# Outputs of narrow experts: from scatter-adds into DRAM to one-hot products added to sums in SBUF

## The chip, the cores and the metric

The kernel runs on one core of one Trainium2 chip. The metric is the time of one execution in device microseconds (us). Three runs of the kernel before took 1312.32 to 1319.89 us, median 1319.34.

## The reference, cut to what matters

One layer (`DEPTH = 1`) of an encoder on 512 tokens of width 1024: a mixer (sparse and differential attention), cross-attention into 256 memory tokens, and a mixture of experts, each followed by a LayerNorm. The change lies in the experts. Each token goes to 8 of 64 SwiGLU experts:

```python
scores = jax.nn.sigmoid(xf @ router_w)
_, top_e = lax.top_k(scores + router_bias, TOP_K)            # 8 of 64
gates = top_s / jnp.sum(top_s) * ROUTED_SCALE
# per block of rows of one expert e, rows = its tokens, g = their gates
yb = (silu(xb @ w_gate[e]) * (xb @ w_up[e])) @ w_down[e] * g   # 1024 -> 256 -> 1024
acc = acc.at[rows].add(yb)
out = acc + shared_expert(x);   h = layer_norm(ALPHA * h + out)
```

All is float32; the weights of one expert are three matrices of 1 MB.

## The kernel before, in words

The kernel is one program of five engines. A small planner (`schedule`) interleaves generator threads; every `yield a, b` gives a time estimate, and a scheduler then sets each engine's own instruction order. The dense stages fill the first 600 us; from then on the thread `experts` runs one block of rows after another.

Experts are ranked by how many tokens chose them, and each rank has a fixed capacity (`CAPS`): 128 rows for the fullest, then 112, 96, 80, 64 and 48. Two ranks have 160 rows and make two blocks, one of 128 and one of 32 rows; `BIG_AT = (30, 50)` says at which steps of the sequence they stand. So there are 64 steps and 66 blocks.

There are two kinds of block. A **wide** one (over 64 rows, or the second part of a 160-row expert) splits its gate and up weights into a high and a low part (ScalarE, VectorE; `split_w`) and multiplies in three products (`mm3`, lines 101 to 103, `expert_mm`). A **narrow** one (64 or 48 rows; `narrow_block`) multiplies plain float32, gate and up side by side in the two halves of a PSUM bank (`narrow_mm`, line 1280). Either way a block goes: gather of its rows from DRAM (`gather`, line 1220, GpSimd queue), transposes (line 1268 for narrow), gate and up products, SiLU on ScalarE (line 1299, tile `sg`), product with up and gate weight on VectorE (line 1304, `hm`), transposes of `hm` (line 1313) and their copy (line 1315, `ht`), the down product (line 1291 for narrow, 1327 for wide). The last three belong to the block before: `narrow_block` finishes block m-1 between its own products. The result is copied to a tile `y` by ScalarE (line 1294) and added to rows of the DRAM tensor `acc` by an indirect DMA that accumulates (`scatter`, line 1332, GpSimd queue). Two scatters must not overlap, so each waits for the one before to land.

Before the experts the shared expert's output and the residual are stored to `acc` (line 1374). After the last scatter, and a loop over experts that overflow their capacity (no turn with these inputs), `acc` is loaded (line 1625, tile `h`) and the last LayerNorm runs on it (lines 171 to 188, 263 to 269, 1639) and stores the output.

Weights are loaded by SyncE's queue (`load_p`, `load_w`, lines 1226 and 1235). `top_up` keeps it `LEAD = 9` loads (three experts) ahead of the block in work. A load's target is one of 20 slots of 8 KB per partition that all large tiles share: raw weights, split weights, `y`.

Of the kernel before, what the change touches and what calls it, by code (L numbers as in the profile page):

```python
# [10 lines left out]
F32 = mybir.dt.float32  # L11
# [8 lines left out]
P = 128  # L20
SEQ = 512
# [18 lines left out]
AHEAD, LEAD = 2, 9  # L40
BIG_AT = (30, 50)
GRP = 4
# [16 lines left out]
def encoder_layer(  # L59
# [16 lines left out]
    def slot(shape, dt=F32, name="s"):  # L76
        return slots.tile(shape, dt, tag="s", name=name)
# [4 lines left out]
    def bank(name="ps"):  # L82
        return psum.tile([P, 512], F32, tag="ps", name=name)
# [1198 lines left out]

    def narrow_out(m, ht, wd, n):

        if m % 2 == 0:
            Y["y"] = slot([P, 2, D], name="y")
        y = Y["y"][:, m % 2, :]
        ps = bank()
        for j in range(2):
            for c in range(2):  # L1290
                nc.tensor.matmul(ps[HALF * c:HALF * c + n, :], lhsT=ht[:, j, 0:n], rhs=wd[:, j, c * 512:(c + 1) * 512],
                                 start=j == 0, stop=j == 1)
        for c in range(2):
            nc.scalar.copy(y[0:n, c * 512:(c + 1) * 512], ps[HALF * c:HALF * c + n, :])
        return y

# [184 lines left out]
    def finish(m, ht, n, wd, si):  # L1481
        if narrow(m):
            y = narrow_out(m, ht, wd, n)
        else:
            for c in range(2):
                y = expert_out(m, ht, wd, c, n)
        scatter(y, si, n)

# [5 lines left out]
    def narrow_block(m, X, xt, gs, si):  # L1494
        r, _, n, _ = blocks[m]
        step = 3 * step_of[r]
        ps = bank()
        w = W[r]
        narrow_mm(xt, w, n, ps, range(KH))
# [3 lines left out]
        yield 0.9, 0.0  # L1503
# [12 lines left out]
    def experts():  # L1516
# [73 lines left out]
    with tc.For_i(0, left, 1) as k:  # L1590
# [83 lines left out]
```

## Time and profile before

| | before |
|---|---|
| runs, median (range) | 1319.34 us (1312.32 to 1319.89) |
| profiled execution, time | 1310.08 us |
| its span, first to last instruction | 1308.3 us |
| busy: PE, PEld, DVE, ACT, POOL | 1155.8, 908.2, 748.5, 562.0, 439.5 us |
| HBM read, written | 288.10 MB, 35.19 MB |

PE is TensorE's matmuls, PEld its weight loads, DVE VectorE, ACT ScalarE, POOL GpSimd, SP SyncE (which only issues DMAs here). A matmul's row lasts from its start to its modelled end, and the next one starts before that end. DMA is the mean busy share of the core's 16 DMA engines. q0 is the queue of the indirect DMAs (gathers and scatters), q1 that of SP.

### The profile page before, as it was taken

How to read it: one execution, taken by the hardware profiler on the slowest of the kernel's cores; microseconds unless marked ns; L12 is line 12 of the kernel's file. 1: busy time of each engine (PE TensorE's matmuls, PEld its weight loads, DVE VectorE, ACT ScalarE, POOL GpSimd, SP SyncE). 2: the span in 40 equal slices, each digit the busy share in tenths (PEclk: the TensorE clock that was granted, in tenths of full speed). 3: DMA queues.
4: the chain of work that ended last, by engine and by line, in shares of the span. 5: the costliest groups of instructions: out<-in, count | busy, mean ns of one | idle time of the engine just before them, and what ended most of it. 6: DMA issues, size and time to landing. Idle time of an engine off the chain costs nothing. (4 is left out here: it accounts for less than half of the span.)

```text
span 1308.3 us, 20859 instructions
## 1 busy us (share of the span) xinstructions
PE 1155.8 (88%) x7768; PEld 908.2 (69%) x7768; DVE 748.5 (57%) x1617; ACT 562.0 (43%) x1006; POOL 439.5 (34%) x288
## 2 busy tenths in 40 slices
PE   3999999999898899889999999999899988897770
PEld 2887778988898898878778777777667544553330
DVE  7168986566865557787767777666465211311114
ACT  3235456644454453335555556555454211321122
POOL 4333444542236343552212323232213222223213
PEclk9999999998999899999999999999999989998995
DMA  7322234463326256688999999999999999999974
GB/s 225 86 74 65 58 103 114 121 202 116 126 67 210 63 185 208 226 332 329 299 289 331 352 347 362 332 359 359 350 367 338 350 347 387 363 363 353 349 279 141
DMA packets 136807, 324.67 MB, mean 248 GB/s; under 512 B 12001, under 2 KB 94945, under 8 KB 111873
## 3 DMA queue, kind: packets, MB, share of 16 engines
q1 hardware_dynamic: 119984, 275.83, 58.2%
q0 software_dynamic: 13632, 46.80, 14.8%
q8 instruction: 62, 1.02, 0.3%
q10 hardware_dynamic: 3088, 0.69, 0.2%
q14 instruction: 41, 0.33, 0.1%
HBM read 288.10 MB, written 35.19 MB: 247 GB/s over the span
## 5 line engine op out<-in xcount | busy, mean ns | idle before, releaser
L95 POOL TENSOR_TENSOR whl<-wraw,whl 128x1024 fp32r<-128x1024 f32 x81 | 195.9, 2419 | 265.4 <-ACT whl L94 239.4
L1244 DVE TENSOR_TENSOR whl<-wraw,whl 128x1024 fp32r<-128x1024 f32 x152 | 182.9, 1231 | 85.7 <-ACT whl L1243 79.6
L1332 POOL DMA_INDIRECT acc<-y,sidx x66 | 104.8, 1587 | 361.5 <-DMA acc<-y,sidx 161.4
L101 PE MATMUL ps<-whl,xt 128*96 128x256 f32 (+4 forms) x640 | 184.3, 288 | 5.6 <-ACT whl L1243 3.9
L103 PE MATMUL ps<-whl,xt 128*96 128x256 f32 (+4 forms) x640 | 179.8, 281 | 1.9 <-DVE xt L95 1.9
L102 PE MATMUL ps<-whl,xt 128*96 128x256 f32 (+4 forms) x640 | 179.6, 281 | 0.6 <-DVE whl L1244 0.6
L1243 ACT CAST whl<-wraw 128x1024 fp32r<-128x1024 f32 x152 | 152.5, 1053 | 27.9 <-DMA wraw<-in_e_w_gate_dram 20.0
L1327 PE MATMUL ps<-wd,ht 128*96 128x512 f32 (+4 forms) x320 | 147.1, 603 | 4.0 <-DVE ht L1315 3.8
L1280 PE MATMUL ps<-wraw,xn 128*64 128x256 f32 (+1 forms) x832 | 116.8, 404 | 27.0 <-DMA wraw<-in_e_w_up_dram 12.2
L1220 POOL DMA_INDIRECT xg<-rows,gidx x66 | 76.5, 1159 | 160.3 <-PE ps L1252 62.5
L1299 ACT ACTIVATE sg<-ps 64x256 f32<-64x256 f32 (+6 forms) x66 | 25.0, 378 | 239.6 <-PE ps L1280 127.1
L94 ACT CAST whl<-wraw 128x1024 fp32r<-128x1024 f32 x91 | 95.4, 1048 | 57.1 <-PE ps L103 46.5
L101 PEld LDWEIGHTS ps<-whl,xt 128*96 128x96 f32 (+4 forms) x640 | 104.3, 163 | 6.8 <-ACT whl L1243 4.1
L103 PEld LDWEIGHTS ps<-whl,xt 128*96 128x96 f32 (+4 forms) x640 | 104.3, 163 | 2.9 <-DVE xt L95 2.6
L1280 PEld LDWEIGHTS ps<-wraw,xn 128*64 128x64 f32 (+1 forms) x832 | 60.6, 140 | 65.0 <-DMA wraw<-in_e_w_up_dram 15.8
L102 PEld LDWEIGHTS ps<-whl,xt 128*96 128x96 f32 (+4 forms) x640 | 104.5, 163 | 1.1 <-DVE whl L1244 0.7
L1327 PEld LDWEIGHTS ps<-wd,ht 128*96 128x96 f32 (+4 forms) x320 | 49.5, 164 | 72.9 <-issue 66.0
L1315 DVE COPY ht<-ps 128x128 f32<-128x128 f32 (+6 forms) x66 | 21.4, 324 | 96.3 <-PE ps L1313 96.3
L1328 ACT COPY y<-ps 96x512 f32<-96x512 f32 (+4 forms) x80 | 46.3, 582 | 68.8 <-PE ps L1327 67.4
L1304 DVE SCALAR_TENSOR_TENSOR hm<-ps,og,sg 64x256 f32<-64x256 f32 (+4 forms) x54 | 36.8, 681 | 58.0 <-ACT sg L1299 48.8
L101 PE MATMUL ps<-xTh,whl 128*128 128x512 f32 (+1 forms) x168 | 65.6, 390 | 0.0
L103 PE MATMUL ps<-xTh,whl 128*128 128x512 f32 (+1 forms) x168 | 63.8, 380 | 0.0
(421 smaller groups left out, 2756.7 us busy)
## 6 DMA issues: line engine op xcount, KB each, us to landing
wraw<-in_e_w_gate_dram SPq DMA_DIRECT2D x64, 1024.0 KB, 18.8
wraw<-in_e_w_up_dram SPq DMA_DIRECT2D x64, 1024.0 KB, 15.7
wd<-in_e_w_down_dram SPq DMA_DIRECT2D x64, 1024.0 KB, 18.0
wraw<-in_w_in_dram SPq DMA_DIRECT2D x21, 512.0 KB, 3.7
wraw<-in_m_wkv_dram SPq DMA_DIRECT2D x16, 512.0 KB, 4.2
wraw<-in_m_wq_dram SPq DMA_DIRECT2D x16, 512.0 KB, 3.9
wraw<-in_m_wo_dram SPq DMA_DIRECT2D x16, 512.0 KB, 3.9
wraw<-in_w_o_dram SPq DMA_DIRECT2D x12, 512.0 KB, 3.5
```

Source lines behind the costliest of these rows:

```text
L94: nc.scalar.copy(hi, src)
L95: eng.tensor_sub(lo, src, hi.bitcast(F32))
L101: nc.tensor.matmul(ps, lhsT=a, rhs=b, start=start, stop=False)
L102: nc.tensor.matmul(ps, lhsT=a, rhs=bl, start=False, stop=False)
L103: nc.tensor.matmul(ps, lhsT=al, rhs=b, start=False, stop=stop)
L1220: nc.gpsimd.indirect_dma_start(out=xg[0:n, :], out_offset=None, in_=rows, in_offset=bass.IndirectOffsetOnAxis(ap=gi[0:n, :], axis=0))
L1243: nc.scalar.copy(hi[v], w[i][v])
L1244: lo_eng.tensor_sub(lo[v], w[i][v], hi[v].bitcast(F32))
L1280: nc.tensor.matmul(ps[HALF * i:HALF * i + n, 0:256], lhsT=xt[:, k, 0:n], rhs=w[i][:, k, :], start=k == 0, stop=k == KD - 1)
L1327: nc.tensor.matmul(ps[0:n, :], lhsT=ht[:, j, 0:n], rhs=wd[:, j, cs], start=j == 0, stop=j == 1)
L1328: nc.scalar.copy(y[0:n, cs], ps[0:n, :])
L1332: nc.gpsimd.indirect_dma_start(out=acc, out_offset=bass.IndirectOffsetOnAxis(ap=si[0:n, :], axis=0), in_=y[0:n, :], in_offset=None, comput ...
```

## The change

Narrow blocks no longer scatter. The sequence is reordered so that all 26 narrow blocks come last (`BIG_AT = (22, 32)`) and are taken in 13 pairs, two blocks of up to 64 rows filling the 128 partitions of one tile `yp`. Each result is written to `yp` as a high part (ScalarE) and a low part (VectorE). From the two blocks' token numbers (`si`, cast to float in `stf`) VectorE makes a one-hot matrix of 128 rows by 512 tokens. `add_sums` multiplies it with `yp`: for 4 tiles of 128 tokens and 2 halves of the width, two products (high, low) into one PSUM bank, which VectorE adds to sums in SBUF (`ACC`). These sums are loaded from `acc` once, by the GpSimd queue, at the third narrow block, and the last LayerNorm reads them in place. The 8 groups of a pair are queued (`READY`, `FL`) and taken by `flush`: two groups at two places in each block, from the block after the pair's end, and what is left at the end. In the narrow stage weights are loaded 12 ahead, not 9.

```diff
-BIG_AT = (30, 50)
+BIG_AT = (22, 32)
...
+    def start_sums():
+        OHS[0] = ohs = slot([P, 4, SEQ], F32R, name="ohs")
+        tk = wk([P, SEQ], name="tk")
+        nc.gpsimd.iota(tk, pattern=[[1, SEQ]], base=0, channel_multiplier=0, allow_small_or_imprecise_dtypes=True)
+        nc.vector.tensor_copy(ohs[:, 0, :], tk)
+
+    def load_sums():
+        for u in range(2):
+            a = slot([P, 2, D], name="sums")
+            for t in range(2):
+                nc.gpsimd.dma_start(a[:, t, :], acc[(2 * u + t) * P:(2 * u + t + 1) * P, :])
+                ACC.append(a[:, t, :])
+
+    def one_hot_rows(oh, stf):
+        nc.vector.tensor_scalar(oh, OHS[0][:, 0, :].bitcast(F32), stf, None, op0=OP.is_equal)
+
+    def add_sums(oh, yp):
+        for t in range(NT):
+            for c in range(2):
+                cs = slice(c * 512, (c + 1) * 512)
+                ps = bank()
+                for l in range(2):
+                    nc.tensor.matmul(ps, lhsT=oh[:, t * P:(t + 1) * P], rhs=yp[:, l, cs], start=l == 0, stop=l == 1)
+                nc.vector.tensor_add(ACC[t][:, cs], ACC[t][:, cs], ps)
+                yield
...
-    def narrow_out(m, ht, wd, n):
-        if m % 2 == 0:
-            Y["y"] = slot([P, 2, D], name="y")
-        y = Y["y"][:, m % 2, :]
+    def narrow_out(m, ht, wd, n, si):
+        i = m - M0
+        p, base = i // 2, HALF * (i % 2)
+        if i % 2 == 0:
+            PAIR[p] = slot([P, 2, D], F32R, name="yp")
+            STF[p] = small.tile([P, 1], F32, name="stf", bufs=3)
+            if min(blocks[m][2], blocks[m + 1][2]) < HALF:
+                nc.vector.memset(STF[p], -1.0)
+        yp, stf = PAIR[p], STF[p]
+        r = slice(base, base + n)
+        if n < HALF:
+            nc.gpsimd.memset(yp[base + 32:base + HALF].bitcast(F32), 0.0)
         ps = bank()
...
+        nc.scalar.copy(stf[r], si[0:n])
         for c in range(2):
-            nc.scalar.copy(y[0:n, c * 512:(c + 1) * 512], ps[HALF * c:HALF * c + n, :])
-        return y
+            cs, v = slice(c * 512, (c + 1) * 512), ps[HALF * c:HALF * c + n, :]
+            nc.scalar.copy(yp[r, 0, cs], v)
+            nc.vector.tensor_sub(yp[r, 1, cs], v, yp[r, 0, cs].bitcast(F32))
+        if i % 2:
+            oh = OHS[0][:, 1 + p % 3, :]
+            one_hot_rows(oh, STF.pop(p))
+            READY.append(add_sums(oh, PAIR.pop(p)))
...
     def top_up(used):
         ahead = 16 + used // 2 if "listed" in done else 0
-        while fetched[0] < min(max(used + LEAD, ahead), 3 * NEXP):
+        lead = LEAD + (3 if used > 3 * step_of[blocks[M0][0]] else 0)
+        while fetched[0] < min(max(used + lead, ahead), 3 * NEXP):
...
         narrow_mm(xt, w, n, ps, range(KH))
         yield 0.45 * KH, 0.0
         ht = expert_h(*BEFORE[0][0:2])
+        flush(2)
         narrow_mm(xt, w, n, ps, range(KH, KD))
...
             X[m + 1] = rows_x(m + 1)
-        yield 0.8, 0.0
+        flush(2)
+        yield 1.6, 0.0
...
         finish(NB - 1, expert_h(*BEFORE[0][0:2]), *BEFORE[0][1:])
+        FL.extend(READY)
+        flush(16)
...
-    h3 = [slot([P, 2, D], name="h") for _ in range(2)]
-    for t in range(NT):
-        nc.sync.dma_start(h3[t // 2][:, t % 2, :], acc[t * P:(t + 1) * P, :])
...
-        h = h3[t // 2][:, t % 2, :]
+        h = ACC[t]
```

The overflow loop's body is changed in the same way (it has no turn here).

How this moves instructions, at three places. First PE, the last narrow blocks and the end: before (line 1268 transposes of gathered rows, 1280 gate and up, 1313 transposes of `hm`, 1291 down product),

```order
L1268 MATMUL ps<-ident,xg 128x48 x8
L1280 MATMUL ps<-wraw,xn 48x256
L1313 MATMUL ps<-ident,hm 128x48 x2
L1291 MATMUL ps<-wd,ht 48x512 x4
L1280 MATMUL ps<-wraw,xn 48x256 x15
L1313 MATMUL ps<-ident,hm 128x48 x2
L1291 MATMUL ps<-wd,ht 48x512 x4
L1589 TENSOR_LOAD rt
```

and with the change (1366 is the old 1313, 1330 the old 1291, 1310 the one-hot products):

```order
L1268 MATMUL ps<-ident,xg 128x48 x8
L1310 MATMUL ps<-yp,ohs 128x512 x4
L1280 MATMUL ps<-wraw,xn 48x256 x12
L1366 MATMUL ps<-ident,hm 128x48 x2
L1310 MATMUL ps<-yp,ohs 128x512 x4
L1280 MATMUL ps<-wraw,xn 48x256 x4
L1330 MATMUL ps<-wd,ht 48x512 x4
L1310 MATMUL ps<-yp,ohs 128x512 x4
L1366 MATMUL ps<-ident,hm 128x48 x2
L1330 MATMUL ps<-wd,ht 48x512 x4
L1310 MATMUL ps<-yp,ohs 128x512 x24
L1655 TENSOR_LOAD rt
```

Each block has gained 8 products of 512 columns, 4 of them between the transposes of its rows and its first product, and 24 stand after the last down product.

Second POOL, the queue of gathers (1220) and scatters (1332). Before, the end of the kernel,

```order
L1220 DMA xg<-rows,gidx 48x1024
L1332 DMA acc<-y,sidx 640x1024
L1220 DMA xg<-rows,gidx 48x1024 x2
L1332 DMA acc<-y,sidx 640x1024 x2
L1220 DMA xg<-rows,gidx 48x1024 x2
L1332 DMA acc<-y,sidx 640x1024
L1220 DMA xg<-rows,gidx 48x1024
L1332 DMA acc<-y,sidx 640x1024 x7
```

and with the change the whole narrow stage (1385 is the last wide scatter, 1297 the load of the sums, 1326 the zeroing of empty rows):

```order
L1385 DMA acc<-y,sidx 640x1024
L1220 DMA xg<-rows,gidx 64x1024 x2
L1297 DMA sums<-acc 128x1024 x4
L1220 DMA xg<-rows,gidx 64x1024 x12
L1220 DMA xg<-rows,gidx 48x1024 x6
L1326 MEMSET yp 32x2048
L1220 DMA xg<-rows,gidx 48x1024
L1326 MEMSET yp 32x2048 x6
```

Scatters no longer stand between the gathers, and four loads and seven fills are new.

Third DVE at the end: before,

```order
L1315 COPY ht<-ps 128x2x48
L1304 SCALAR_TENSOR_TENSOR hm<-ps,og,sg 48x128x2
L1271 COPY xn<-ps 128x4x48
L1315 COPY ht<-ps 128x2x48
L1304 SCALAR_TENSOR_TENSOR hm<-ps,og,sg 48x128x2
L1315 COPY ht<-ps 128x2x48
L1589 TENSOR_LOAD rt
```

and with the change (1368 is the old 1315, 1311 an addition to the sums, 1336 the low part of `yp`):

```order
L1311 TENSOR_TENSOR sums<-sums,ps 128x512
L1368 COPY ht<-ps 128x2x48
L1336 TENSOR_TENSOR yp<-ps,yp 48x512
L1311 TENSOR_TENSOR sums<-sums,ps 128x512
L1336 TENSOR_TENSOR yp<-ps,yp 48x512
L1311 TENSOR_TENSOR sums<-sums,ps 128x512 x2
L1336 TENSOR_TENSOR yp<-ps,yp 48x512
L1311 TENSOR_TENSOR sums<-sums,ps 128x512 x9
L1655 TENSOR_LOAD rt
```

Behind the last `ht` copy VectorE now has 3 low parts and 12 additions to do.

## Rows read from the trace of the kernel before

**Rows 1.** The page: span, and busy share of the DMA engines in 40 slices.
```profile
span 1308.3 us, 20859 instructions
...
DMA  7322234463326256688999999999999999999974
```

**Rows 2.** Stages: us; busy PE, PEld, DVE, ACT, POOL; clock, DMA share, GB/s.
```profile
602.00:1010.00 408.00, 393.91 (x2707) 307.00 (x2706) 274.18 (x509) 219.69 (x330) 111.82 (x74) 0.99 1.00 343
1010.00:1268.00 258.00, 218.16 (x1471) 116.08 (x1469) 50.60 (x148) 56.00 (x117) 60.72 (x51) 0.93 1.01 357
1268.00:1308.30 40.30, 1.92 (x8) 0.43 (x8) 14.67 (x27) 8.61 (x14) 14.03 (x12) 0.59 0.42 124
```

**Rows 3.** DMA queues, 1107 to 1112 us: packets, MB, share of 16 engines.
```profile
q1 hardware_dynamic: 292, 2.13, 100.8%
```

**Rows 4.** DMA queues, 1216.5 to 1219.0 us: one scatter of 64 rows.
```profile
q0 software_dynamic: 70, 0.26, 52.5%
```

**Rows 5.** DMA queues, 1092.3 to 1094.6 us: one gather of 64 rows.
```profile
q0 software_dynamic: 63, 0.25, 35.3%
```

**Rows 6.** Timeline of PE, one narrow block: start, us, what, [idle before <-releaser].
```profile
1044.39 2.81 PE L1280 MATMUL ps<-wraw,xn 128*64 128x256 f32 x24 [0.26 <-ACT xn L1273]
...
1048.31 1.89 PE L1291 MATMUL ps<-wd,ht 128*64 128x512 f32 x8
1050.12 0.71 PE L1268 MATMUL ps<-ident,xg 64*128 64x64 f32 x8
1051.86 2.81 PE L1280 MATMUL ps<-wraw,xn 128*64 128x256 f32 x24 [1.03 <-ACT xn L1273]
```

**Rows 7.** Timeline of PE: products of 512 columns of split operands, back to back.
```profile
100.11 0.40 PE L101 MATMUL ps<-xTh,whl 128*128 128x512 f32 x1
...
100.81 0.40 PE L101 MATMUL ps<-xTh,whl 128*128 128x512 f32 x1
```

**Rows 8.** Groups by line and shape: VectorE and ScalarE operations; last numbers busy us, mean ns.
```profile
L1294 ACT COPY y<-ps 64x512 f32<-64x512 f32 x38 | 22.0, 579 | 8.6 <-PE ps L1291 8.3
L1304 DVE SCALAR_TENSOR_TENSOR hm<-ps,og,sg 64x256 f32<-64x256 f32 x19 | 12.8, 672 | 24.7 <-ACT sg L1299 24.6
L95 DVE TENSOR_TENSOR x<-ps,x 128x512 fp32r<-128x512 f32 x16 | 10.4, 677 | 0.0
L1271 DVE COPY xn<-ps 128x256 f32<-128x256 f32 x19 | 8.1, 424 | 47.9 <-PE ps L1268 47.9
L1315 DVE COPY ht<-ps 128x128 f32<-128x128 f32 x19 | 5.5, 291 | 61.5 <-PE ps L1313 61.5
```

**Rows 9.** Line 1280 on PE: all narrow gate and up products, first and last start.
```profile
L1280 PE MATMUL ps<-wraw,xn x832: 378/379/688, 1011.4 to 1266.0; 128*64 128x256 f32 x122, 128*48 128x256 f32 x45
```

**Rows 10.** Timeline of ACT: SiLU before and in the second 160-row expert's two blocks.
```profile
1126.34 0.38 ACT L1299 ACTIVATE sg<-ps 64x256 f32<-64x256 f32 x1 [2.97 <-PE ps L1280]
...
1145.02 0.37 ACT L1299 ACTIVATE sg<-ps 32x256 f32<-32x256 f32 x1 [5.06 <-PE ps L103]
```

**Rows 11.** Timeline of PE: after the first 160-row expert's second block.
```profile
949.77 0.42 PE L1313 MATMUL ps<-ident,hm 32*128 32x32 f32 x2 [4.71 <-DVE sidx L1185]
```

**Rows 12.** Timeline of the end, all engines.
```profile
1266.43 0.38 ACT L1299 ACTIVATE sg<-ps 48x256 f32<-48x256 f32 x1 [2.27 <-PE ps L1280]
1268.23 1.92 PE L1291 MATMUL ps<-wd,ht 128*48 128x512 f32 x8 [0.35 <-DVE ht L1315]
1270.20 1.17 ACT L1294 COPY y<-ps 48x512 f32<-48x512 f32 x2 [3.39 <-PE ps L1291]
...
1286.57 1.76 SPq L1625 DMA_DIRECT2D h<-acc  x4
1289.92 0.69 DVE L171 BATCH_NORM_STATS2 st<-h 128x6 f32<-128x512 f32 x1 [21.74 <-DMA h<-acc]
```

**Rows 13.** The chain that ended last: start, us, what; the last scatter.
```profile
1281.80 4.05 DMA acc<-y,sidx
```

**Rows 14.** Waits of SP's queue, 1010 to 1268 us: total us, times, longest.
```profile
SPq L1235 <- DMA wraw<-in_e_w_gate_dram: 48.2, 17, 3.7
```

More of the change, by code (lines that the diff above doesn't have):

```diff
@@ L1292, in narrow_out, with flush @@
                                  start=j == 0, stop=j == 1)
+        nc.scalar.copy(stf[r], si[0:n])
         for c in range(2):
-            nc.scalar.copy(y[0:n, c * 512:(c + 1) * 512], ps[HALF * c:HALF * c + n, :])
-        return y
+            cs, v = slice(c * 512, (c + 1) * 512), ps[HALF * c:HALF * c + n, :]
[5 more added lines that the diff above has]
+            READY.append(add_sums(oh, PAIR.pop(p)))
+    def flush(n):
+        while n and FL:
+            if next(FL[0], 0) == 0:
+                FL.pop(0)
+            else:
+                n -= 1
     def expert_gate(pg, n=P):
@@ L1395, in encoder_layer @@
     NB = len(blocks)
+    M0 = min(m for m in range(NB) if blocks[m][2] <= HALF and not blocks[m][1])
+    assert all(blocks[m][2] <= HALF and not blocks[m][1] for m in range(M0, NB)) and (NB - M0) % 2 == 0
     W, XG, GS = {}, {}, {}
@@ L1482, in finish @@
         if narrow(m):
-            y = narrow_out(m, ht, wd, n)
+            narrow_out(m, ht, wd, n, si)
         else:
@@ L1486, in finish @@
                 y = expert_out(m, ht, wd, c, n)
-        scatter(y, si, n)
+            scatter(y, si, n)
     def rows_x(m):
@@ L1496, in narrow_block @@
         step = 3 * step_of[r]
+        if m == M0 + 1:
+            start_sums()
+        if m == M0 + 2:
+            load_sums()
         ps = bank()
         w = W[r]
+        FL.extend(READY)
+        READY.clear()
         narrow_mm(xt, w, n, ps, range(KH))
@@ L1501, in narrow_block @@
         ht = expert_h(*BEFORE[0][0:2])
+        flush(2)
         narrow_mm(xt, w, n, ps, range(KH, KD))
-        yield 0.9, 0.0
+        yield 1.8, 0.0
         top_up(step + 2)
@@ L1565, in experts @@
         finish(NB - 1, expert_h(*BEFORE[0][0:2]), *BEFORE[0][1:])
+        FL.extend(READY)
+        flush(16)
     for u in range(2):
@@ L1616, in encoder_layer @@
         ht = expert_h(expert_mid(expert_gate(pg), pu, gs))
-        for c in range(2):
-            y = expert_out(0, ht, w3[2], c)
-        scatter(y, si)
+        stf = small.tile([P, 1], F32, name="stf", bufs=3)
+        nc.vector.tensor_copy(stf, si)
+        oh = OHS[0][:, 1, :]
+        one_hot_rows(oh, stf)
+        yp = slot([P, 2, D], F32R, name="yp")
+        for c in range(2):
+            cs = slice(c * 512, (c + 1) * 512)
+            ps = bank()
+            for j in range(2):
+                nc.tensor.matmul(ps, lhsT=ht[:, j, :], rhs=w3[2][:, j, cs], start=j == 0, stop=j == 1)
+            split(yp[:, 0, cs], yp[:, 1, cs], ps)
+        for _ in add_sums(oh, yp):
+            pass
     gb = G3[0]
-    h3 = [slot([P, 2, D], name="h") for _ in range(2)]
-    for t in range(NT):
-        nc.sync.dma_start(h3[t // 2][:, t % 2, :], acc[t * P:(t + 1) * P, :])
     st = []
     for t in range(NT):
-        h = h3[t // 2][:, t % 2, :]
+        h = ACC[t]
         if t % 2:
@@ L1634, in encoder_layer @@
     for t in range(NT):
-        h = h3[t // 2][:, t % 2, :]
+        h = ACC[t]
         mu, rs = st[t]
```

1 line of the change is left out of this document (added).

## The prediction

> **What bounds the kernel now.** I read the page first. Its DMA row stands at 9 from about 650 us to nearly the end [rows 1]: two thirds of the run load expert weights, 64 x 3 MB. The table by stage then divides this stretch [rows 2]. In the wide stage (602 to 1010 us) both limits are met: PE is busy 393.91 of 408 us, and the DMA share is 1.00. In the narrow stage (1010 to 1268) the DMA share is 1.01, while PE is busy 218.16 of 258 at a mean granted clock of 0.93, so part of it ran at the lower of the two levels. So the transfers end last there, and PE has room. The third piece, 1268 to 1308.3, is the end: PE does 1.92 us in it, so this is latency.
>
> Next I asked the DMA queues for short stretches, to see what a scatter costs the engines. Weights alone use them fully at 2.13 MB in 5 us, or 426 GB/s [rows 3]. One scatter of 64 rows takes 52.5% of 2.5 us, or 1.31 us of all 16 engines, for 0.26 MB [rows 4]. The same bytes gathered take 35.3% of 2.3 us, 0.81 us [rows 5]. So the thing removed is the dearest traffic per byte.
>
> At the end, the last SiLU starts at 1266.43, the last down product ends at 1268.23 + 1.92 = 1270.15, and the first LayerNorm instruction starts at 1289.92 [rows 12]. Between them the late scatters run one after another (the last one 4.05 us from issue to landing [rows 13]), then `acc` is loaded from 1286.57 on.
>
> **The change, part by part.** The sum is made against the profiled execution: span 1308.3 us [rows 1], its own time 1310.08, which is under all three runs (1312.32 to 1319.89). I take the difference to the median, 1319.34.
>
> *Scatters out of the narrow stage.* Of 26 narrow blocks (19 of 64 rows, 7 of 48) the last four scatter after the last SiLU. In the stage lie 19 x 1.31 + 3 x 0.98 (three quarters) = 27.8 us of transfer time. *Sums in:* 2 MB, eight times a gather's bytes, between 4.9 us at 426 GB/s and 6.5 at a gather's price; I take 5.5. They stand on POOL's queue and wait for the last wide scatter; behind them wait gathers that are fetched two blocks ahead, so a scatter's 4.05 us or twice that is covered. Transfers: -22.3 us.
>
> *Products in.* 13 pairs x 16 = 208 products of 512 columns. Such products follow each other at (100.81 - 100.11) / 3 = 0.23 us [rows 7], so 3.7 us a pair, 1.85 a block, 48 in all. They are PE work in a stage where PE had 258 - 218 = 40 us free [rows 2], part of it waits for transfers that go away.
>
> How long is a narrow block on PE? One that had its weights took 1051.86 - 1044.39 = 7.47 us from first product to first product, 1.03 of them idle for ScalarE's copy of the next rows [rows 6]. The change puts 4 products (0.92 us) right into that gap. So 7.47 - 0.92 + 1.85 = 8.4 us.
>
> *The 160-row expert moved forward.* Its two blocks took 1145.02 - 1126.34 = 18.7 us in the narrow stage [rows 10], where transfers went on below them. In the wide stage PE has no room, so they push the first narrow product from 1011.4 [rows 9] to about 1030. The first such expert also stalled PE for 4.71 us just after [rows 11]; a second stall is bounded by 0 and a little more than that one, and I take 4.7, as the place is of the same kind: 1034.8.
>
> *Two floors for the last SiLU*, 1266.43 before. PE: 1034.8 + 25 blocks x 8.4 + 5 us of the last block's products = 1250, -16.5. Transfers: -22.3, and if the engines idle through the second stall too, +4.7 = -17.6. They nearly meet, and where both meet neither is reached: the wide stage, with both full, left PE 14 of 408 us idle [rows 2]; the same 3.5% of 215 us is 7. Stage: -16.5 + 7 = **-9.5 us**, ends -22 and +5.
>
> *VectorE and ScalarE.* ScalarE copies as before (0.58 us each). VectorE gains, per block, 4 additions and 2 low parts, nearest row a 128x512 subtraction from PSUM at 0.677, and half a one-hot row (0.3): 4.4 us. With `hm` 0.672, `xn` 0.424 and `ht` 0.291 [rows 8] that is 5.8 of 8.4 us. It is hidden by the block's own products as long as `ht` and `xn` come in time. POOL's seven fills and one iota (POOL was busy 60.7 of 258 us) cost nothing, bounded by a ScalarE copy that waits for a fill; so do the small casts.
>
> *12 ahead.* Zero. SP already waits for earlier loads to land, in such rows as 17 times for 48.2 us in all [rows 14]: the loads are issued faster than they land, and asking earlier adds no bandwidth. If it helps, the rival of free transfers below holds it.
>
> *The end.* Up to 1270.15 nothing changes. ScalarE's two copies end at 1270.20 + 1.17 = 1271.4, the low part follows (0.68), then 9 of the 12 additions: 1272.05 + 9 x 0.677 = 1278.1. PE's last 24 products need 24 x 0.23 = 5.5 us and are ahead of them; at half clock 11 us, to 1281.2. From a landed scatter to the next instruction took 1286.57 - 1281.80 - 4.05 = 0.7 us. First LayerNorm instruction at 1278.8 against 1289.92: **-11 us**, ends -8 and -12. The LayerNorm itself, 18.4 us, stays.
>
> Sum: -9.5 - 11 = -20.5 us; 1308.3 becomes 1288 for the span, and the median 1319.34 becomes **1299 us**.
>
> A rule to weigh: the Trainium skill, "Perfetto Trace Analysis", section "Identifying the Most-Contended Engine", says that matmul busy time tells little of PE's headroom and that the busy share of weight loads is the better measure. In the narrow stage that share is 116.08 of 258, or 45% [rows 2]; by that rule the 48 us of products would find room without cost, and the outcome would be the first rival's. The block that had its weights and still took 7.47 us [rows 6] speaks against it.
>
> **Rivals.**
>
> *Transfers alone decide.* The products fall into PE's waits, and the moved expert costs nothing since the engines load ahead below it. For it: PE's 40 free us, and the lower clock in the stage, which a busier PE would not see. Against: the 7.47 us. Then the stage gives its whole -22.3, the end -11: **1286 us**.
>
> *The stage gives nothing.* The moved expert's 18.7 us and stalls in the full wide stage, with slots too few to load ahead (the sums, one-hot rows and pairs hold five of the 20), eat what the scatters gave. For it: PE's 14 free us of 408 there. Then only the end is won: **1308 us**.
>
> *The products block PE's queue.* PE works in order. A product waits for a PSUM bank that an addition frees, and that addition stands on VectorE behind low parts that wait for ScalarE's copies of the same block. Two such waits of about 1 us (an addition and a half) make the block 10.4 us, and the last SiLU comes at 1034.8 + 25 x 10.4 + 5 = 1300, +33; with -11 at the end, **1342 us**, slower. It decides from about 9.5 us a block on (1277.4 for the last SiLU eats the end's gain). For it: VectorE at 5.8 of 8.4 us and 2 of the 4 places of products in a pair right behind the copies. Against: eight banks, a block's products in between, and 40 us of PE's room.
>
> *That it does not do what it says* I see only for the 12 ahead, priced at zero above.
>
> **How the numbers follow.** Chances: forecast 0.5 (own range 1289 to 1310), transfers alone 0.17, no gain in the stage 0.2, blocked queue 0.13. The predicted time is the forecast's, 1299. The range leaves out half of the first rival's far side and the most of the last one's: 1281 to 1319. About 1% (13 us, a time of 1306) is what a measurement of this kernel can tell. Faster by more: 0.8 of the forecast, the first rival, a fifth of the second: 0.61. Within 1%: 0.1 of each side's rest, the second rival's bulk and a mild blocked queue: 0.27. Slower: 0.12.
>
> **What would show it.** In the changed profile: the first narrow product near 1030 to 1035; from SiLU to SiLU 8.4 to 8.8 us in the narrow blocks, with a granted clock near 1; the DMA share still near 1 in the stage, with q0's part down by half; the last SiLU near 1257 and 12 us from it to the first LayerNorm instruction. I am wrong if PE idles on VectorE's additions (blocked queue), if SiLUs come 9.5 us apart or more, if the first narrow product is later than 1045, or if the end has kept 20 us.

## The result, and the profile after

The changed kernel takes 1373.05 us (median of 4 runs, 1365.61 to 1380.10) against 1319.62 for the kernel before, timed with it: ratio 1.041, 95% interval 1.034 to 1.048. It is slower by 53 us, where the prediction had it 20 us faster.

The profiled execution took 1375.24 us, 65 more than the one of before. The page of the kernel after, first its span, TensorE's granted clock and the DMA engines in 40 slices, then the queue of gathers and scatters:

```profile
span 1373.4 us, 21439 instructions
...
PEclk9999999999999999999999999899999989999995
DMA  7221234464243357889999999999999998878601
...
q0 software_dynamic: 12240, 42.54, 12.4%
```

The DMA row no longer stands at 9 to the end [rows 1]: from 1130 us on it is at 8, 7 and 6. q0 kept the engines busy for 12.4% of 1373 us, 170 us, against 14.8% of 1308, 194 us: 23 us less. The forecast's 22.3 counts only the 22 scatters ahead of the last SiLU; at its prices all 26 come to 31.8 us, less 5.5 for the sums 26. So the transfers did go, nearly as forecast, and something else fills the time.

Stages of the kernel after, cut at the first narrow product and the last SiLU: us, busy PE, PEld, DVE, ACT, POOL, clock, DMA share, GB/s.

```profile
602.00:1044.00 442.00, 424.62 (x2933) 331.34 (x2932) 289.29 (x547) 232.86 (x355) 120.60 (x82) 0.99 0.99 335
1044.00:1331.00 287.00, 255.28 (x1473) 123.46 (x1473) 138.17 (x271) 50.11 (x121) 36.18 (x34) 0.93 0.79 287
1331.00:1373.40 42.40, 10.73 (x46) 5.78 (x40) 27.22 (x46) 9.77 (x17) 9.25 (x8) 0.67 0.13 50
```

The narrow stage took 287 us, though it has lost the second 160-row expert; before it had 258 with it [rows 2]. Its DMA share fell to 0.79, and PE was not full either. Neither limit is met: the stage waits. The first narrow product comes 33 us later than before [rows 9]:

```profile
L1280 PE MATMUL ps<-wraw,xn x832: 379/379/431, 1044.5 to 1330.2; 128*64 128x256 f32 x122, 128*48 128x256 f32 x45
```

Of these 33 us, 5.7 lie ahead of the experts, in code that the change does not touch: the SiLU of the very first expert block came at 608.58 in this execution and at 602.85 in that of before. In the runs below that keep the kernel before in all but one point (e3, e8, e15) it came at 609.8, 607.6 and 609.4, and in one with the change (e12) at 603.1, so this belongs to the execution and not to the change.

What does the stage wait for? ScalarE's timeline over two blocks of the kernel after (start, us, what, [idle before <-releaser]; line 1352 is the SiLU, 1335 the copy to the high part of `yp`):

```profile
1110.88 0.38 ACT L1352 ACTIVATE sg<-ps 64x256 f32<-64x256 f32 x1 [6.13 <-PE ps L1280]
...
1118.38 0.38 ACT L1352 ACTIVATE sg<-ps 64x256 f32<-64x256 f32 x1 [2.42 <-PE ps L1280]
1118.66 1.17 ACT L1335 CAST yp<-ps 64x512 fp32r<-64x512 f32 x2
1120.44 1.30 ACT L1335 CAST yp<-ps 64x512 fp32r<-64x512 f32 x2 [0.61 <-DVE yp L1336]
...
1135.06 0.38 ACT L1352 ACTIVATE sg<-ps 64x256 f32<-64x256 f32 x1 [6.13 <-PE ps L1280]
```

After the SiLU at 1110.88 there is no copy; after the next come four, those of both blocks of a pair. And PE in the same stretch (line 1310 a one-hot product, 1330 the down product):

```profile
1119.89 0.50 PE L1310 MATMUL ps<-yp,ohs 128*128 128x512 f32 x1 [1.57 <-ACT yp L1335]
1121.18 1.41 PE L1310 MATMUL ps<-yp,ohs 128*128 128x512 f32 x2 [0.79 <-DVE yp L1336]
1122.52 3.68 PE L1330 MATMUL ps<-wd,ht 128*64 128x512 f32 x6
1126.12 0.80 PE L1310 MATMUL ps<-yp,ohs 128*128 128x512 f32 x1
1126.85 1.22 PE L1330 MATMUL ps<-wd,ht 128*64 128x512 f32 x2
...
1134.82 1.89 PE L1330 MATMUL ps<-wd,ht 128*64 128x512 f32 x8
```

The pair's first product stands on PE ahead of the down product and waits for the copy that ScalarE has only just done. After two such waits the down product takes 3.68 us for six matmuls, where eight take 1.89 one block later. The granted clock was 0.50 there, the lower of its two levels (1.2 instead of 2.4 GHz); over 50 us it was 0.84 of full speed:

```profile
1121.00:1126.00 5.00, 4.82 (x8) 1.33 (x8) 2.20 (x4) 0.60 (x2) 0.00 (x0) 0.50 1.01 421
1100.00:1150.00 50.00, 45.41 (x237) 21.34 (x236) 23.10 (x46) 8.18 (x20) 3.58 (x4) 0.84 0.98 367
```

From start to start that is 0.60 us a matmul against 0.23, 2.6 times as long, which half the clock does not explain in full. The SiLUs of the stage come in pairs here, 16.7 and 7.5 us apart, 12 us a block.

The waits of the whole narrow stage (engine, line waited for: us in total, times, longest), first PE's matmuls, then its weight loads, then SP's queue:

```profile
PE ps L1310 <- ACT yp L1335: 20.3, 10, 3.1
PE ps L1310 <- DVE yp L1336: 6.4, 10, 0.8
PE ps L1310 <- DVE sums L1311: 0.5, 1, 0.5
```
```profile
PEld ps L1310 <- ACT yp L1335: 28.9, 20, 3.6
```
```profile
SPq L1226 <- PE ps L1280: 89.5, 21, 5.8
SPq L1235 <- PE ps L1330: 81.0, 17, 9.3
```

The products wait for ScalarE's copies; for VectorE's additions the matmuls wait 0.5 us in all. (A wait of a weight load and one of the product behind it can be the same time, so the two lists are not added.) SP, which before waited for earlier loads to land [rows 14], now waits for PE to give slots back. So PE is late, and the transfers wait for it.

The end of the kernel after (line 1311 an addition to the sums, 263 the LayerNorm, 1715 the stores):

```profile
1330.63 0.38 ACT L1352 ACTIVATE sg<-ps 48x256 f32<-48x256 f32 x1 [4.56 <-PE ps L1280]
1335.11 1.92 PE L1330 MATMUL ps<-wd,ht 128*48 128x512 f32 x8 [1.42 <-DVE ht L1368]
1341.22 5.47 DVE L1311 TENSOR_TENSOR sums<-sums,ps 128x512 f32<-128x512 f32 x9
1347.48 1.06 ACT L263 ACTIVATE sq<-sums 128x1024 f32<-128x1024 f32 x1 [7.72 <-DVEq L1656]
```

From the last SiLU to the first LayerNorm instruction it is 16.85 us, against 23.5 before [rows 12]. But from the SiLU to the end of the span it is 42.8 against 41.9. Most of that is the last wait: SP saw the last store landed at 1366.36, and GpSimd reported only at 1372.66, after a DRAIN of 11.13 us that began at 1361.48; before, that DRAIN took 4.06 us and was over ahead of the stores. (DRAIN is a control instruction near the end of an engine's program; the trace records it, the views leave it out.)

### The profile page after: what moved, and what is told of

The parts are those of the page before. It is cut to its first block, busy times and chain, and to the rows that moved or that the text cites. A ratio compares the mean times of both kernels' runs of the same rounds, so it can differ in the third digit from the quotient of the medians.

```text
span 1373.4 us, 21439 instructions
## 1 busy us (share of the span) xinstructions
PE 1232.5 (90%) x7976; PEld 943.9 (69%) x7976; DVE 857.1 (62%) x1791; ACT 566.5 (41%) x1032; POOL 416.7 (30%) x274
## 3 DMA queue, kind: packets, MB, share of 16 engines
q0 software_dynamic: 12240, 42.54, 12.4%
## 5 line engine op out<-in xcount | busy, mean ns | idle before, releaser
L1220 POOL DMA_INDIRECT xg<-rows,gidx x66 | 71.3, 1080 | 355.8 <-PE ps L1268 227.9
L1385 POOL DMA_INDIRECT acc<-y,sidx x40 | 72.0, 1800 | 201.6 <-DMA acc<-y,sidx 80.7
L1280 PE MATMUL ps<-wraw,xn 128*64 128x256 f32 (+1 forms) x832 | 101.7, 385 | 0.8 <-ACT xn L1273 0.8
L1310 PE MATMUL ps<-yp,ohs 128*128 128x512 f32 x208 | 73.6, 456 | 28.1 <-ACT yp L1335 20.3
L1311 DVE TENSOR_TENSOR sums<-sums,ps 128x512 f32<-128x512 f32 x104 | 67.5, 684 | 49.5 <-PE ps L1310 38.0
L1280 PEld LDWEIGHTS ps<-wraw,xn 128*64 128x64 f32 (+1 forms) x832 | 53.7, 133 | 39.1 <-issue 13.2
L1310 PEld LDWEIGHTS ps<-yp,ohs 128*128 128x128 f32 x208 | 37.2, 194 | 63.0 <-ACT yp L1335 29.3
L1330 PE MATMUL ps<-wd,ht 128*64 128x512 f32 (+1 forms) x208 | 74.7, 702 | 4.3 <-DVE ht L1368 4.3
```

Of the source, the lines that this page charges most:

```text
L1280: nc.tensor.matmul(ps[HALF * i:HALF * i + n, 0:256], lhsT=xt[:, k, 0:n], rhs=w[i][:, k, :], start=k == 0, stop=k == KD - 1)
L1310: nc.tensor.matmul(ps, lhsT=oh[:, t * P:(t + 1) * P], rhs=yp[:, l, cs], start=l == 0, stop=l == 1)
L1385: nc.gpsimd.indirect_dma_start(out=acc, out_offset=bass.IndirectOffsetOnAxis(ap=si[0:n, :], axis=0), in_=y[0:n, :], in_offset=None, comput ...
```

## The experiments

Theory 1 grew out of the timelines: `yp` is a tile in the 20 shared slots, asked for once per pair, behind the weight loads that `top_up` has just asked for. Slots are given in the order of asking. With 12 loads ahead they are all taken, so `yp` comes late, and with it the copies of both blocks. Theory 2: the products and additions themselves hold PE. Theory 3: part of the loss is in the wide stage, from the moved 160-row experts.

All ratios are to the kernel before, timed on the same chip; intervals are 95%. The kernel before took 1318.7 to 1319.9 us (medians) in these timings, so times of different groups can be set side by side to about 1 us.

| run | us, median | ratio, interval |
|---|---|---|
| the change | 1373.05 | 1.0409, 1.0335 to 1.0484 |
| e1_own_yp | 1341.77 | 1.0151, 1.0117 to 1.0184 |
| e2_lead9 | 1359.24 | 1.0287, 1.0255 to 1.0319 |
| e3_big_at | 1331.28 | 1.0092, 1.0058 to 1.0126 |
| e4_own_lead9 | 1335.27 | 1.0105, 1.0064 to 1.0147 |
| e5_down_first | 1322.83 | 1.0039, 1.0017 to 1.0062 |
| e6_sums_on_sp | 1328.88 | 1.0078, 1.0048 to 1.0108 |
| e7_big_later | 1322.94 | 1.0057, 1.0025 to 1.0089 |
| e8_before_lead12 | 1327.36 | 1.0080, 1.0054 to 1.0105 |
| e9_pe_order_kept | 1307.75 | 0.9909, 0.9877 to 0.9941 |
| e10_no_iota | 1308.89 | 0.9936, 0.9912 to 0.9961 |
| e11_all | 1307.49 | 0.9918, 0.9894 to 0.9942 |
| e12_one_product | 1298.56 | 0.9851, 0.9819 to 0.9883 |
| e13_drain_early | 1306.29 | 0.9897, 0.9860 to 0.9933 |
| e14_gpsimd_dma | 1308.89 | 0.9900, 0.9868 to 0.9932 |
| e15_before_reordered | 1313.91 | 0.9961, 0.9933 to 0.9989 |

**e1_own_yp: two buffers of its own for `yp`.**

```diff
         OHS[0] = ohs = slot([P, 4, SEQ], F32R, name="ohs")
+        YP.extend(slot([P, 2, D], F32R, name="yp") for _ in range(2))
...
-            PAIR[p] = slot([P, 2, D], F32R, name="yp")
+            PAIR[p] = YP[p % 2]
```

> The change, but with two buffers for the converted outputs of a pair (yp) taken once, instead of one asked for per pair behind the weights that are loaded 12 ahead; nothing else. Theory 1 (the copies to yp come late because yp gets its buffer only when the weights asked for before it have theirs, so that products stand on PE waiting for ScalarE): the copies of a block come in the block after it, the waits of the products on them (25.1 us on the weight loads and 17.3 us on PE after the change) fall under 10 us, a block takes 8.4 to 9.3 us instead of 12, and 25 intervals from the first SiLU of the narrow stage to the last take 210 to 235 us instead of 282: 1300 to 1326 us. Theory 2 (the products and additions themselves hold PE, wherever the copies stand): the blocks stay near 12 us, 1360 to 1380 us.

1341.77 us, 31 us faster than the change, but between the ranges of the two theories. ScalarE's program order shows what the edit did (S a SiLU, y a copy to `yp`, x the copy of the next rows; the middle of the narrow stage):

```
change   Sx Syyyyx Sx Syyyyx Sx Syyyyx Sx Syyyyx
e1       Syxy Syxy Syxy Syxy Syxy Syxy Syxy Syxy
```

PE in two blocks of e1 (lines are one higher than after: 1311 a one-hot product, 1331 the down product):

```profile
1126.82 1.89 PE L1331 MATMUL ps<-wd,ht 128*64 128x512 f32 x8
1128.64 0.71 PE L1268 MATMUL ps<-ident,xg 64*128 64x64 f32 x8
1129.28 1.21 PE L1311 MATMUL ps<-yp,ohs 128*128 128x512 f32 x4
1130.42 2.81 PE L1280 MATMUL ps<-wraw,xn 128*64 128x256 f32 x24
...
1135.47 1.89 PE L1331 MATMUL ps<-wd,ht 128*64 128x512 f32 x8
```

No wait stands in them, and a block takes 1135.47 - 1126.82 = 8.65 us, with all its products. From 1060 to 1300 us PE's products waited 1.6 us for ScalarE (17.2 after the change), its weight loads 2.5 (24.8). Theory 1 holds, and theory 2 falls for these blocks. But the stage's 25 intervals took 1303.9 - 1055.7 = 248 us, more than the 235 expected: two of them, from 1089 us on, took 13.7 and 15.6, where ScalarE's order still had the copies of two blocks behind one SiLU, and from 1162 us on the blocks took 9.4 to 13.2.

**e2_lead9: 9 ahead instead of 12, `yp` as in the change.**

```diff
-        lead = LEAD + (3 if used > 3 * step_of[blocks[M0][0]] else 0)
+        lead = LEAD
```

> The change with narrow weights 9 ahead instead of 12, yp still asked for per pair. Theory 1: three fewer weights stand before yp, the copies of about half of the pairs come a block earlier, and half of the loss in the narrow stage goes: 1330 to 1352 us. Theory 2 (the products hold PE): 1360 to 1380 us. A third theory, that 12 ahead keeps the transfers going through the stage: slower than the change, above 1380 us.

1359.24 us: 14 faster than the change, 7 above the range of theory 1. In the trace the blocks take 6.8 to 10.7 us until 1152, and then the pairs of 15.8 and 7.9 us are back. Fewer loads ahead move the point from which `yp` is late; they do not remove it. That 12 ahead helps the transfers is out.

**e3_big_at: the kernel before with only the 160-row experts moved.**

```diff
-BIG_AT = (30, 50)
+BIG_AT = (22, 32)
```

> The kernel before with the two 160-row experts at steps 22 and 32 instead of 30 and 50, nothing else. By the prediction's sum the second one only changes its place: 23.4 us more in the wide stage and as much less in the narrow one, 1315 to 1324 us. Theory 3 (it costs more in the wide stage, since a buffer held by a scatter stalls the weight conversion of its neighbour, 8.78 us of PE's wait at 871 us after the change): first narrow SiLU 30 to 34 us later than before, 1325 to 1333 us.

1331.28 us, 12 us slower, in the range of theory 3. In its trace the narrow stage is 18.1 us shorter (232.8 against 250.9 from first to last SiLU), the wide one 29.5 longer (to the first narrow product, less 7.0 that lie ahead of the experts as above), just under the 30 of theory 3, where 23.4 were forecast. The stall after the first such expert is 8.9 us here; in the kernel after, its row and the one on ScalarE that stands behind it (line 1243 splits weights) are

```profile
871.61 0.42 PE L1366 MATMUL ps<-ident,hm 32*128 32x32 f32 x2 [8.78 <-DVE sidx L1185]
```
```profile
868.48 3.89 ACT L1243 CAST whl<-wraw 128x1024 fp32r<-128x1024 f32 x4 [9.75 <-DMA acc<-y,sidx]
```

ScalarE's split waits for a slot that a scatter still reads; PE's next products need the split. So the stall is a shortage of slots too, 8.8 us at step 22 against 4.7 at step 30 [rows 11]. Theory 3 holds in its time: the moved experts cost the wide stage 29.5 us and gave back 18.1 in the narrow one, which transfers bound. The stall is only 4.2 of the difference.

**e4_own_lead9: e1 with 9 ahead.** The edit is e1's and e2's together.

> e1 with narrow weights 9 ahead instead of 12. Theory 1 says that what 12 ahead did was to stand before yp, which no longer matters: the same as e1 within 8 us, 1298 to 1328 us. If 12 ahead keeps the transfers going, e1 is the faster by 10 us or more.

1335.27 us, 6.5 less than e1, just inside the 8 us, though 7 above the range given for the time. With buffers of its own `yp` does not care much for 12 or 9 ahead. The slower second half of the stage stays. PE there (a piece of one block):

```profile
1173.47 1.20 PE L1311 MATMUL ps<-yp,ohs 128*128 128x512 f32 x4
1174.97 1.50 PE L1331 MATMUL ps<-wd,ht 128*64 128x512 f32 x5 [0.30 <-DVE ht L1369]
1175.88 0.59 PE L1280 MATMUL ps<-wraw,xn 128*64 128x256 f32 x2
1176.31 0.59 PE L1331 MATMUL ps<-wd,ht 128*64 128x512 f32 x1
1176.32 3.39 PE L1280 MATMUL ps<-wraw,xn 128*64 128x256 f32 x27
1179.38 0.59 PE L1331 MATMUL ps<-wd,ht 128*64 128x512 f32 x1
```

PE's order is not that of 1126 us: the transposes of `hm` and most of the down product stand ahead of the gate and up products, the rest among them, and in some blocks PE waits up to 1.64 us for `ht`, which VectorE does behind a low part and a one-hot matrix.

**e5_down_first: the down product of the block before moved ahead in the program, 10 ahead, no zeroing of `yp`.**

```diff
-        narrow_mm(xt, w, n, ps, range(KH))
         ht = expert_h(*BEFORE[0][0:2])
         flush(2)
-        narrow_mm(xt, w, n, ps, range(KH, KD))
+        finish(m - 1, ht, *BEFORE[0][1:])
+        narrow_mm(xt, w, n, ps, range(0, KD))
         top_up(step + 2)
         sg = expert_gate(ps, n)
-        finish(m - 1, ht, *BEFORE[0][1:])
...
-        if n < HALF:
-            nc.gpsimd.memset(yp[base + 32:base + HALF].bitcast(F32), 0.0)
```

> e4 with 10 ahead, the down product and the conversion of the block before ahead of the gate and up products on PE (in e4 they stand among them from 1150 us on, and blocks go from 8.6 to 9.4 and 10.3 us), and without the zeroing of unused rows of yp on GpSimd (they hold old numbers, and their one-hot rows are zero). If the place in PE's order is what costs these blocks 0.8 to 1.7 us: 18 intervals near 8.6 us and 7 near 10 us, last SiLU 10 to 16 us earlier than in e4, 1317 to 1327 us. If DVE's work or the transfers hold a block at 9.4 us: 1331 to 1339 us as e4. GpSimd's last DRAIN, 11.13 us in all kernels with the change and 4.06 us in those without: 4 us if the zeroing set it, else as it was.

1322.83 us, as expected of the order. In the trace most blocks take 8.5 us, and the last eight 9.7 to 10.8: from the 19th block on the transposes of the next block and four products stand among the gate and up products, ahead of all but the first two, and PE waits for `hm` with nothing left to do ([1.17 <-DVE hm L1356] in the first two). The DRAIN took 11.13 us again, so the zeroing does not set it. What 10 ahead instead of 9 did is not told apart from the order here.

**e6_sums_on_sp: the sums loaded by SP's queue.**

```diff
-                nc.gpsimd.dma_start(a[:, t, :], acc[(2 * u + t) * P:(2 * u + t + 1) * P, :])
+                nc.sync.dma_start(a[:, t, :], acc[(2 * u + t) * P:(2 * u + t + 1) * P, :])
```

> e5 with the loads of the sums issued from SP's queue instead of GpSimd's. If these loads are what lengthens GpSimd's last DRAIN: 4 us in its place and 6 to 7 us less in all; else the DRAIN stays at 11.1 us. The weights behind the loads in SP's queue wait for the last scatter of a wide expert: 0 to 5 us more at 1060 to 1075 us if that is not hidden.

1328.88 us, and a DRAIN of 10.81: the loads are not its cause. The blocks at 1060 to 1090 us are as quick as in e5, so the wait in SP's queue was hidden. The 6 us are elsewhere: the scheduler placed the transposes ahead of the products from the 14th block on, not from the 19th.

**e7_big_later: e5 with the 160-row experts at steps 30 and 36.**

```diff
-BIG_AT = (22, 32)
+BIG_AT = (30, 36)
```

> e5 with the 160-row experts at steps 30 and 36 instead of 22 and 32. If the 8.8 us of PE's wait at the first of them come from ScalarE's wait for a buffer that a scatter still reads, which 30 does not have (4.7 us in the kernel before): 4 to 9 us faster than e5. If it is only that two blocks more of PE's work stand in a stage that PE bounds: the same as e5 within 3 us.

1322.94 us, the same. The stall fell to 5.9 us (9.2 in e5), but the time did not: a block of the narrow stage took 12.3 us instead, at a DMA share of 1.02 (1085 to 1100 us). So the stall saved in the wide stage was given back where the transfers were full; what ended that block's wait the trace does not show.

**e8_before_lead12: the kernel before with 12 ahead in the narrow stage.**

```diff
-        while fetched[0] < min(max(used + LEAD, ahead), 3 * NEXP):
+        while fetched[0] < min(max(used + LEAD + (3 if used > 3 * step_of[NARROW0] else 0), ahead), 3 * NEXP):
```

> The kernel before with narrow weights 12 ahead instead of 9, nothing else. The prediction priced 12 ahead at zero: 1312 to 1326 us. If it takes buffers that outputs need in the kernel before too: 5 to 15 us slower. If it smooths the transfers: 5 to 10 us faster.

1327.36 us, 9 us slower than the 1318.70 timed with it, in the range of the second expectation. ScalarE's order again (y now a copy to the `y` that is scattered):

```
before         Syyx Syyx Syyx Syyx Sxyy Syyx Sx Sxyyyy Sx
before, 12     Syyx Syyx Sx Sxyyyy Sx Sx Sxyyyy Sx Sxx
```

Late copies stood in the kernel before too, and 12 ahead adds more of them. There only a scatter waits for them, so they cost little; the change put PE behind them.

**e9_pe_order_kept: e5 with PE's order tied.**

```diff
+        with tc.issue_after(last.ins):       # the block's last gate/up product
-        if m + 1 < NB:
-            X[m + 1] = rows_x(m + 1)
-        flush(2)
+            if m + 1 < NB:
+                X[m + 1] = rows_x(m + 1)
+            flush(2)
```

> e5 with the transposes of the next block and the second half of the products tied behind the last gate and up product on PE, so that they stand there in all 26 blocks (in e5 they stood ahead of it in the last 7 blocks, which took 10.3 us with a wait of 1.17 us for hm). If the order alone cost that: 25 blocks near 8.5 us, last SiLU 11 to 13 us earlier than in e5, 1308 to 1315 us. If the weights are late there: the blocks stay over 9.5 us with waits on the loads, 1318 to 1326 us.

1307.75 us: faster than both kernels, 0.9% (0.6 to 1.2) faster than the one before. Small as it is, this is clear of the noise. Two blocks of its narrow stage (1312 a one-hot product), and the stage:

```profile
1187.02 3.65 PE L1280 MATMUL ps<-wraw,xn 128*64 128x256 f32 x32
1190.60 0.71 PE L1268 MATMUL ps<-ident,xg 64*128 64x64 f32 x8
1191.24 1.19 PE L1312 MATMUL ps<-yp,ohs 128*128 128x512 f32 x4
1192.37 0.33 PE L1366 MATMUL ps<-ident,hm 64*128 64x64 f32 x2
1192.63 1.21 PE L1312 MATMUL ps<-yp,ohs 128*128 128x512 f32 x4
1193.82 1.94 PE L1330 MATMUL ps<-wd,ht 128*64 128x512 f32 x8
1195.56 3.65 PE L1280 MATMUL ps<-wraw,xn 128*64 128x256 f32 x32
```
```profile
1051.00:1270.00 219.00, 213.68 (x1467) 130.56 (x1466) 127.91 (x269) 51.48 (x123) 23.92 (x28) 1.00 1.00 366
```

PE does not idle in the block shown, which takes 1195.56 - 1187.02 = 8.54 us. The stage is 219 us with the DMA share at 1.00 and PE at 214: both limits met at once.

**e10_no_iota: e9 without the late iota on GpSimd.**

```diff
-        nc.gpsimd.iota(tk, pattern=[[1, SEQ]], base=0, channel_multiplier=0, allow_small_or_imprecise_dtypes=True)
-        nc.vector.tensor_copy(ohs[:, 0, :], tk)
+        for t in range(NT):
+            nc.vector.tensor_scalar(ohs[:, 0, t * P:(t + 1) * P], slot_id[:, 0:P], float(t * P), None, op0=OP.add)
```

> e9 with the row of token numbers made by four additions on DVE from a row that is there already, instead of an iota on GpSimd at 1042 us. If the iota is what lengthens GpSimd's last DRAIN from 4.06 to 11.13 us: 4 us there and 6 to 7 us less in all, 1301 to 1309 us; else as e9.

1308.89 us and a DRAIN of 11.13: not the iota.

**e11_all: e10 with the 160-row experts at 30 and 36.** The edit is e7's.

> e10 with the 160-row experts at steps 30 and 36. In e7 the first narrow SiLU came 6 to 7 us earlier than in e5 by that, and the last only 1 us, since a block at 1087 us waited. If transfers bound the stage by now: as e10 within 3 us. If PE does: 4 to 7 us faster, 1295 to 1305 us.

1307.49 us, as e10: the first expectation. Its narrow stage is 215.5 us, both limits met:

```profile
1049.00:1264.50 215.50, 212.42 (x1466) 128.96 (x1465) 128.01 (x270) 51.27 (x123) 23.17 (x27) 1.00 0.99 365
```

**e12_one_product: e11 with one piece in eight of the products** (so the sums lack most of the narrow experts).

```diff
+                if t == 0 and c == 0:      # around the products and the addition
```

> e11 with one of the eight pieces of the products and additions of a pair (seven are left out, so that most of the sums lacks the narrow experts). 2.26 us a block less on PE, 6.3 instead of 8.5 us. If PE bounds the narrow stage: 25 blocks at 6.5 to 7.5 us, 25 us or more faster than e11. If transfers bound it as soon as the order is right: blocks at 8.0 to 8.4 us and 3 to 12 us faster, apart from the end, where 24 products and 12 additions fall out (8 us).

1298.56 us, 9 less than e11. The stage:

```profile
1043.00:1255.30 212.30, 178.82 (x1308) 96.56 (x1306) 84.22 (x193) 51.42 (x122) 23.17 (x27) 0.98 1.01 369
```

34 us less of PE's busy time shorten the stage by 3 us: transfers bound it at once, as the second expectation has it. Until 1168 us most blocks take 7.4 to 7.7 us, then mostly 8.8 and more. The rest is at the end (41.3 us from the last SiLU in e11, 33.7 here). So in the right order the products cost about 3 us of the stage and 8 at the end, by the traces; the medians are 9 apart.

**e13_drain_early, e14_gpsimd_dma: GpSimd's last DRAIN.** In e13 VectorE does GpSimd's half of the last row tile, in e14 GpSimd issues a small store just ahead of the LayerNorm.

```diff
-            scale_add(v, v, rs, b, c == 0)
+            scale_add(v, v, rs, b, c == 0 and t < NT - 1)         # e13
...
+    nc.gpsimd.dma_start(acc[SEQ:SEQ + 16, :], gb[0:16, 0, :])    # e14
```

> e11 with the last row tile of the final LayerNorm finished on DVE, where GpSimd does half of it in e11. If GpSimd's last DRAIN takes its 9.6 us from GpSimd's last work on: it begins 3 to 4 us earlier and the end comes 3 to 5 us earlier, DVE's added 0.7 us against it: 1302 to 1306 us. If the DRAIN ends a fixed time after the stores: as e11.

> e11 with a store of 16 unused rows issued from GpSimd's queue just ahead of the final LayerNorm. If the DRAIN is long because GpSimd's queue had issued no DMA for 60 us, where the kernel before issued its last scatter 20 us before the DRAIN: 4 us instead of 11.1. Else 11 us as before, 1304 to 1312 us.

e13: 1306.29 us; the time does not tell it from e11, the trace does: the DRAIN is over 9.6 us after the end of GpSimd's last operation in both (1297.46 to 1307.04, and in e11 1295.33 to 1304.90), and from the last SiLU to the end of the span it is 37.7 us instead of 41.3. It is a time after GpSimd's last work, as the first expectation had it. e14: 11.21 us. Its store went out at 1261.17, 35 us ahead of the DRAIN at 1295.90, not 20 as in the kernel before, where the last scatter was issued at 1281.80 and the DRAIN began at 1301.26. So a DMA 35 instead of 62 us old (e11) changes nothing, and one 20 us old is untested. From GpSimd's last operation to the end of the DRAIN the kernel before takes 2.1 us (1303.18 to 1305.32). What makes that longer in all kernels with the change stays open.

**e15_before_reordered: the kernel before with PE's order of e9**, edits as in e5 and e9, without products.

> The kernel before with PE's order of e9 in the narrow blocks (down product of the block before first, transposes of the next tied behind the last gate and up product); scatters, 9 ahead and the steps 30 and 50 as they were. If the gain of e9 to e11 is that order's: 1305 to 1312 us. If transfers bound the narrow stage of the kernel before, as the prediction read it: 1314 to 1324 us.

1313.91 us, just under the range of the second expectation: the order alone brings 0.4% (0.1 to 0.7). e11, at 0.8% (0.6 to 1.1), and e9 and e13, at 0.9 and 1.0%, have more than that, though the intervals overlap a little: some 0.5% is left for the change itself, and it is shown only weakly. Its narrow stage is still bound by transfers:

```profile
1025.00:1278.00 253.00, 207.15 (x1449) 114.94 (x1447) 46.63 (x142) 55.76 (x116) 59.32 (x50) 0.94 1.02 358
```

## Why the prediction was wrong

**Right.** The transfers: q0 fell by 23 us, where the forecast's prices make 26. The block on PE, once nothing waits: forecast 8.4 us; 8.65 in e1, 8.54 in e9. One term in it was small: four one-hot products take 1130.42 - 1129.28 = 1.14 us, not 0.92. Inside a group they follow at 0.23 to 0.24, as the split products do [rows 7], but the first and the last of the four are followed only after 0.34 and 0.33, so 208 come to 59 us rather than 48. The two floors that nearly meet: in e9 and e11 they do, and the stage of 214 us from first product to last SiLU in e11 (1050.1 to 1264.4) is a little under the forecast's 222 (1034.8 to 1257).

**The step that failed: "So 7.47 - 0.92 + 1.85 = 8.4 us."** It put the products into a gap as if their operands were there; the wait for the copies to `yp` has no term in the sum. PE takes its queue in order, so a product is a wait as soon as its copies are late, and what stands behind it, the down product and the next block, waits too. From the first narrow product to the last SiLU it took 286 us instead of 222. Of the 64 us between, 26.7 are waits of the products for `yp` (20.3 and 6.4), and the lower clock took up to 20 more (0.07 of 287 us; an estimate from the mean of 0.93). The copies were late because `yp` asks for a slot behind the weight loads: with buffers of its own 31 us came back (e1). The rows could have warned: ScalarE's order in the kernel before already has copies of two blocks behind one SiLU (under e8), harmless as long as only a scatter waits. It was not looked at.

**A second step that failed: "*12 ahead.* Zero."** It was argued from bandwidth alone: asking earlier adds none. But a load also asks for a slot, and `yp` stands behind it in the same 20. The prediction counted those slots only once, under the rival "the stage gives nothing" ("with slots too few to load ahead"), and from the other end: it feared that the pairs would take slots from the loads, where the loads took them from the pairs. 12 instead of 9 ahead cost 9 us with scatters (e8), 14 in the change (e2) and 6.5 once `yp` had its own buffers (e4). So it made the late copies worse, and it was not what made them: with 9 ahead the change still took 1359 us.

**The rival "the products block PE's queue"** had the sign and the place, not the mechanism. It priced waits for additions and PSUM banks; those came to 0.5 us on the matmuls. The waits were for ScalarE's copies (20.3 us on matmuls, 28.9 on weight loads), and the lower clock came with them. Its 10.4 us a block were 12 in the pairs, its 1342 us were 1373.

**The moved expert, "about 1030", then "I take 4.7".** It cost 27.4 us ahead of the narrow stage (33.1 less the 5.7 of the execution), not 23.4. The stall was not what was short: the trace has one, of 8.78 us at step 22, and none like it at the second expert, 4.1 more than the one of before [rows 11], where 4.7 were added. Short were the two blocks themselves. From SiLU to SiLU they took 981.95 - 957.46 = 24.5 us in the wide stage, where 18.7 were carried over from the narrow one [rows 10]:

```profile
957.46 0.38 ACT L1352 ACTIVATE sg<-ps 80x256 f32<-80x256 f32 x1 [1.85 <-PE ps L103]
...
981.95 0.37 ACT L1352 ACTIVATE sg<-ps 32x256 f32<-32x256 f32 x1 [6.54 <-PE ps L103]
```

And the narrow stage gave back less than the wide one paid: 18.1 against 29.5 us in e3, which alone is 12 us slower than the kernel before. e7 and e11 show that the place within the wide stage does not matter.

**"*The end* ... -11 us".** It gave +1.0 in the profiled executions (42.81 us from the last SiLU, against 41.85). The first LayerNorm instruction comes 16.85 us after the last SiLU, not 12.4: PE waits 1.4 us for `ht`, which stands behind an addition and a low part on VectorE, and each copy of a half waits for the low part of the half before. Then "The LayerNorm itself, 18.4 us, stays" failed: 26.0, of which 6.3 are the wait for GpSimd's DRAIN after the last store. No row of before showed that DRAIN, since there it was hidden.

**The rule that was weighed**, of the Trainium skill ("Perfetto Trace Analysis", section "Identifying the Most-Contended Engine"; it names the share of peak arithmetic beside that of weight loads, which is not worked out here), by which the products find room: by e12 they do, nearly, once copies and order are right (3 us of the stage). In the change as it stood they did not, with weight loads busy 123 of 287 us, 43%. A busy share, of either kind, does not see an engine that waits in order.

**Accounted, in medians:** 53 us slower; 12 are the moved experts, if e3's price holds in the change, and the rest is the late copies and PE's order, less the transfers saved. Steps e1, e4, e5 and e9 (31, 6.5, 12.4, 15.1) sum to 65 us and lead to 1308, 1% faster than before. The size forecast, 20 us, was not reached: the best of the runs that keep all products has 13.

## What to carry to other kernels

Before putting work on an in-order engine, find out when its operands are written in the order that exists, not in the order of the program's text: a copy that is harmlessly late for a DMA is a stall for PE. Count slots as well as bytes when loads are asked for earlier, and give a small tile that PE waits for buffers of its own, outside the pool that prefetches fill. Work that stands in a stage bound by transfers costs less there than in a stage that the engine fills: moving the 160-row experts saved 18 us in the one and cost 30 in the other.

## What the runs showed of the hardware

GpSimd's last DRAIN ended 9.2 to 9.7 us after GpSimd's last operation in the kernels with the change, and 2.1 to 2.2 us after it in those without (before, e3, e8, e15). It was neither the zeroing nor the iota nor the loads of the sums; that a DMA of 20 us ago shortens it is not ruled out. The way around it that e13 shows is to let GpSimd finish early.

Two waits of 1.57 and 0.79 us in a block were followed by a down product at a granted clock of 0.50 (3.68 us for six matmuls against 1.89 for eight). So short waits on PE can cost more than their length; in e9, with hardly any, the granted clock is 1.00 over the stage.
